# Whole PSUM bank pairs for each transpose task, and new offsets for the left operands of two projections, in a two-layer decoder trunk

## The chip, the cores and the metric

One core of one Trainium2 chip. The metric is the device time of one execution in microseconds (us), the median of the runs; one further execution was taken with the hardware profiler, and its trace is what the text reads.

## The reference

Two decoder layers over 256 tokens with a model width of 1024 (two token tiles of 128), all in float32:

```python
def layer(x, kind):
    x = x + 0.5 * swiglu(rms_norm(x), w_gate, w_up, w_down)   # ffn1, hidden width 2816
    h = rms_norm(x)
    p = h @ w_in                       # q, k, v of two groups of 8 heads of 64
    # kind 0: stick-breaking heads | block-sparse heads (q, k normed, rope)
    # kind 1: forgetting heads (q, k normed, gate log_f) | dilated-window heads (q, k normed, rope)
    o = concat(group_1(p), group_2(p))
    x = x + o @ w_out
    return x + 0.5 * swiglu(rms_norm(x), w_gate, w_up, w_down)   # ffn2
```

With 256 tokens the block-sparse heads see one block, so they are causal softmax attention. Every product is made to nearly float32 accuracy from parts: each operand is a sum of a rounded `hi` and a rest `lo`, and `hi*hi + lo*hi + hi*lo` are added up.

## The kernel before

**Stages.** The feed-forward stage (`ffn`), the mixing stage (`mix`), the feed-forward stage again, twice. Weights stream through: a DMA on the SP queue brings one unit of 128 x 2048 into `raw` (three buffers), ACT rounds each half to `hi` (L238), DVE takes the difference `lo` (L239; nine buffers each), and then come the matmuls (`mm3`, all recorded at L155 in `mm`). The stationary operand is the activations with the features on the partitions, 128 x 128 a matmul; the moving one is the weights, 128 x 512.

**The gate and up projections** run over blocks of 512 or 384 columns, for two token tiles and eight slices of the model width, into an `acc` bank (gate) and a `z` bank (up). The hidden blocks h are transposed, and ACT and DVE split them into `hh` and `hl` (`split_evac`, L251 and L252). **The down projection** (`row_gemm`) takes `hh` and `hl` as the stationary operand. **The mixing stage** projects q, k and v of the one group, then of the other. q and k of the normed heads go through `norm` (ACT square, DVE sum, POOL power, DVE product, and for rope POOL and DVE products: L475 to L488) and are transposed into `qT`, `kT` (L493). Each group then runs over four pairs of heads: scores into two `z` banks (`soft_a`, `stick_a`), a transposition of the weights (`soft_b`, one head a call) or the cumulative sum as a matmul (`stick_b`), and the product with v into the `o` bank (`c`). `out` splits a finished half into `oh`, `ol`, the stationary operand of the out projection.

**The norm of a stage** (`Normed`). After each half of a token tile's residual, the scaled half `xg` is transposed into `xt`. `inverse` takes the norm, and in the mixes it broadcasts the inverse over the partitions by a matmul with a diagonal matrix, into `rb` (L293 to L297).

**PSUM.** Eight banks of 512 columns: three `acc` in turn, one `o`, two `z`, and one tile `tt` of two banks. `slot()` hands out the two halves of 256 columns of `tt` in turn, each half across both banks:

```python
    tt = psum.tile([P, 2, 512], F32, tag="tt", bufs=1, name="tt")
    def slot():
        slots[0] += 1
        c0 = (slots[0] % 2) * 256
        return tt[:, :, c0:c0 + 256]
```

A task is given one half and the next the other half of the same banks. PE waits before it writes one half until the readers of the other are done, as the rows of its waits show.

**The order of the work.** PE's order is written out by hand: `Weave` keeps an estimated clock `pe.t`, and tasks spawned as generators (transposes, norms, groups of heads) are run from within the streams of matmuls when that clock reaches their time. The leads say how long after its inputs' start a task comes: `LEAD_X` for xt, `LEAD_R` and `LEAD_R0` for rope heads, `LEAD_N` for the others, `LEAD_F` for the forget gate, and `PACE` sets the distance of one head pair to the next. The other engines' order is set by the program's scheduler.

**Start.** The first token tile's halves are scaled and transposed one by one, then the second tile's (`second_tile`), between the first gate matmuls.

Of the kernel before, what the change touches and what calls it, by code (L numbers as in the profile page):

```python
# [28 lines left out]
HD = 64  # L29
# [83 lines left out]
def trunk(ctx, tc, a, out):  # L113
# [14 lines left out]
    def nm(s):  # L128
        seen[s] = seen.get(s, 0) + 1
        return f"{s}_{seen[s]}"  # L130
# [4 lines left out]
    def acc():  # L135
        return bank("acc", 3)
# [25 lines left out]

    def transposes(src, n):

        tb = slot()
        for j in range(n):
            for b in range(2):
                r = slice(b * HP, (b + 1) * HP)
                nc.tensor.transpose(tb[:, b, j * HP:(j + 1) * HP], src[r, j * P:(j + 1) * P], ident[r, r])  # L169
            pe.t += 0.06  # L170
        return tb[:, :, :n * HP].rearrange("p b (c t) -> p c b t", t=HP)

# [39 lines left out]
    def rpow(ss, n, width):  # L212

        m = small.tile([P, width], F32, tag=f"ms{width}", name=nm("ms"))
        nc.vector.tensor_scalar(m, ss, 1.0 / n, EPS, op0=ALU.mult, op1=ALU.add)  # L215
        r = small.tile([P, width], F32, tag=f"rp{width}", name=nm("rp"))
        nc.gpsimd.tensor_tensor(r, m, mhalf[:, :width], op=ALU.pow)  # L217
        return r
# [40 lines left out]
    class Normed:  # L259
# [7 lines left out]

        def start(self, t, h, ps=None, scale=1.0, lead=None, gain=None):
            self.ready[t].append(pe.spawn(self.transpose(t, h, ps, scale, lead or LEAD_X[t][h], gain)))

        def transpose(self, t, h, ps, scale, lead, gain):
            tk, sl, kk = slice(t * P, (t + 1) * P), slice(h * 512, (h + 1) * 512), slice(4 * h, 4 * h + 4)
            if ps is not None:
                residual(ps, t, h, scale)
            xg = xpool.tile([P, 512], F32, tag="xg", bufs=2, name=nm("xg"))
            nc.vector.tensor_mul(xg, x[t][:, sl], self.g[:, sl] if gain is None else gain)
            self.xg[t].append(xg)
            yield lead
            split_evac(transposes(xg, 4), self.hi[:, kk, tk], self.lo[:, kk, tk])
            if h == 1:  # L280
                self.rdone[t] = pe.spawn(self.inverse(t, self.xg[t]))

        def inverse(self, t, junk):
# [9 lines left out]
            nc.gpsimd.tensor_mul(diag, ident, self.r[t].to_broadcast([P, P]))  # L293
# [69 lines left out]
    def ffn(layer, wg, wu, wd, xt, done, between=None):  # L363
        with tc.tile_pool(name=nm("ffn"), bufs=1) as fp:
# [19 lines left out]
            def hidden(hs, c0, n):  # L384
                ft, m = c0 // P, n // P
                vs = [transposes(h, m) for h in hs]
                for t, v in enumerate(vs):
                    split_evac(v, hh[:, ft:ft + m, t * P:(t + 1) * P], hl[:, ft:ft + m, t * P:(t + 1) * P])
                yield 0.0
# [53 lines left out]
    def _mix(mp, layer, xt, gains, done):  # L443
# [23 lines left out]

        def project_norm(c0, g, tag, lead=LEAD_R):
            qT = mp.tile([P, 4, SEQ], F32, tag=tag, bufs=2, name=nm(tag))
            tasks = []  # L470
            rope = isinstance(g, tuple)

            def norm(t, ps):
                sq = new("sq")
                nc.scalar.activation(sq, ps, AF.Square, scale=xt.r[t])  # L475
# [4 lines left out]
                nc.vector.scalar_tensor_tensor(heads(qn), heads(ps), xt.r[t],  # L480
                                               r.unsqueeze(2).to_broadcast([P, 8, HD]), op0=ALU.mult, op1=ALU.mult)
                if rope:
                    gc, gs = g
                    o, sw = new("qs"), new("sq")
                    half_swap(lambda u, v: nc.gpsimd.tensor_mul(  # L485
                        heads(sw)[:, :, u], heads(qn)[:, :, v], over_heads(gs[:, t, u])))
                    nc.vector.tensor_mul(heads(o), heads(qn), over_heads(gc[:, t]))  # L487
                    nc.vector.tensor_add(o, o, sw)  # L488
                    yield lead
                else:  # L490
                    o = qn
                    yield LEAD_N
                nc.scalar.activation(halves(qT[:, :, t * P:(t + 1) * P]), transposes(o, 4), AF.Copy,  # L493
                                     scale=1.0 if rope else g)

            token_major(xt, w, c0, acc, lambda t, ps: tasks.append(pe.spawn(norm(t, ps))))
            return qT, tasks

        def forget():
# [12 lines left out]
            pe.join(*xt.rdone)  # L512
            ps = slot()[:, 0]
            for k in range(KT):
# [4 lines left out]
            def rest():  # L519
# [8 lines left out]
                yield LEAD_F  # L528
                tb = slot()[:, 0]
                for t in range(2):  # L530
# [3 lines left out]
                yield 1.0  # L534
                tb = slot()[:, 0]
                mm(tb[:8, 0:P], lg[:, 0], cv("le"), True)
# [23 lines left out]
        class Group:  # L560
# [11 lines left out]
            def run(self, after, pace, other):  # L572
# [5 lines left out]
                for i in range(4 + 2):  # L578
                    if i < 4:
                        a_(i)  # L580
                    if 0 <= i - 1 < 4:
                        b_(2 * (i - 1))
                        b_(2 * (i - 1) + 1)
                    if 0 <= i - 2 < 4:
# [33 lines left out]

            def stick_b(self, h):
                sp, ls = self.z.pop(h)  # L620
                b = slot()
                mm(b[:, 0], cv("suf"), sp[:, 0:256], True)
                mm(b[:, 0, P:], cv("nones"), sp[:, 256:384], False)
                mm(b[:, 1, :P], cv("suf"), sp[:, 256:384], True)
                nc.vector.tensor_add(ls[:, 0:256], ls[:, 0:256], b[:, 0])
                nc.vector.tensor_add(ls[:, 256:], ls[:, 256:], b[:, 1, :P])
                pT = self.pT[h] = new("pT", 384, 4)
                nc.scalar.activation(pT, ls, AF.Exp)

# [35 lines left out]

            def soft_b(self, h):
                tb = transposes(self.z.pop(h), 3)
                pT = self.pT[h] = new("pT", 384, 4)
                nc.vector.tensor_copy(halves(pT.rearrange("p (c t) -> p c t", t=P)), tb)  # L669

            def c(self, p):
                if p % 2 == 0:
                    self.ob = obank()
                c0 = (p % 2) * SEQ
                pTs = [self.pT.pop(2 * p + s) for s in range(2)]
                for t, (r0, r1) in enumerate(((0, 256), (256, 384))):
                    for s in range(2):
                        o = self.ob[s * HD:s * HD + HD, c0 + t * P:c0 + SEQ]
                        mm(o, self.vs[t][:, (2 * p + s) * HD:(2 * p + s + 1) * HD], pTs[s][:, r0:r1],
                           t == 0 and p % 2 == 0, at_once=2)  # L680
# [27 lines left out]
        gq, gk = gains[0]  # L708
        q2, tq = project_norm(cb, gq, "qT", LEAD_R0)
        k2, tk = project_norm(D + cb, gk, "kT")  # L710
# [30 lines left out]
    def second_tile():  # L741
        load_x(1)
        for h in range(2):
            xt.start(1, h, lead=LEAD_0)

    for h in range(2):
        xt.start(0, h, gain=gb[h])
    first_units.extend([lambda: None, second_tile])
# [47 lines left out]
```

## Time and profile before

| | us |
|---|---|
| median of 3 runs (lowest, highest) | 1087.64 (1087.39, 1088.31) |
| the profiled execution | 1086.83 |
| its span, from the first to the last instruction | 1085.0 |
| mixing stage of layer 0, window in the span | 208.0 to 361.2 |
| mixing stage of layer 1, window in the span | 734.0 to 897.8 |
| mean granted clock of PE | 0.983 |

Times in the rows are microseconds from the start of the span, a mean in a group's row is nanoseconds. PE is the matrix engine, PEld its loading of the stationary operand, DVE, ACT and POOL are the vector, scalar and GpSimd engines, SP the engine that issues the weights' DMAs. A row names output and inputs as the program does: `acc<-hi,xt` adds a product of weights and `xt` to an acc bank. `tt<-ident,...` is a transposition by a matmul with the identity. "L169" is a line of the program above. In a row of the timeline, brackets hold the idle time before the instruction and what ended it.

### The profile page before, as it was taken

The numbers are of one execution on the slowest core, as the hardware profiler recorded it, in microseconds if no ns is written. First come the engines' busy times: TensorE is split into PE (matmuls) and PEld (weight loads), VectorE is DVE, ScalarE is ACT, GpSimd is POOL, SyncE is SP. The second block draws the span as 40 slices with busy tenths as digits, with TensorE's granted clock in tenths as the row PEclk, the third lists the DMA queues.
The fourth block names the chain that finished last, engine by engine and source line by source line (L and its number), as shares of the span: only waits on it lengthen the run. The fifth ranks groups of instructions, "written<-read, shape, count | busy, mean of one in ns | idle before, by whom it ended". The sixth has DMA issues, their size and how long they took to land.

```text
span 1085.0 us, 13584 instructions
## 1 busy us (share of the span) xinstructions
PE 1027.7 (95%) x5412; PEld 841.7 (78%) x5412; DVE 611.6 (56%) x825; ACT 497.8 (46%) x682; POOL 76.1 (7%) x91
## 2 busy tenths in 40 slices
PE   5999999898799999999999999998888989999998
PEld 3888988677676788998788899876755767889986
DVE  5554554666756654564475456447667765555541
ACT  6544543454353644453364445335435544544530
POOL 2000000053000000000010000003431000000000
PEclk9999999999999999999999999999999989999999
DMA  9564665452322564565466456534108316454631
GB/s 327 185 210 128 211 229 180 152 178 97 133 101 78 183 216 135 168 241 185 133 224 216 133 170 242 184 131 161 54 17 281 131 57 215 156 169 164 249 118 39
DMA packets 82657, 178.55 MB, mean 165 GB/s; under 512 B 4993, under 2 KB 21665, under 8 KB 82594
## 3 DMA queue, kind: packets, MB, share of 16 engines
q1 hardware_dynamic: 79776, 174.83, 47.2%
q10 hardware_dynamic: 2818, 2.86, 0.8%
q8 instruction: 42, 0.69, 0.3%
q14 instruction: 21, 0.17, 0.0%
HBM read 176.59 MB, written 1.05 MB: 164 GB/s over the span
## 4 chain that ended last, share of the span: by engine, by line
PE 85%; DVE 8%; ACT 2%; issue 2%; POOL 2%; DMA 1%; SPq 0%; DVEq 0%; ACTq 0%
PE acc L155 51%; PE z L155 24%; PE o L155 6%; DVE lo L239 4%; PE tt L169 3%; ACT hi L238 2%; PE tt L155 1%; POOL rp L217 1%; DMA raw<-in_ffn_w_gate 1%; DMA raw<-in_ffn_w_up 1%; DVE pT L669 1%; DVE mx L653 1%; POOL sq L485 1%; DVE qs L487 0%; DVE x L257 0%
## 5 line engine op out<-in xcount | busy, mean ns | idle before, releaser
L239 DVE TENSOR_TENSOR lo<-raw,hi 128x1024 fp32r<-128x1024 f32 (+1 forms) x344 | 403.0, 1182 | 263.8 <-ACT hi L238 255.7
L238 ACT CAST hi<-raw 128x1024 fp32r<-128x1024 f32 (+1 forms) x344 | 344.1, 1010 | 307.5 <-PE z L155 134.1
L155 PE MATMUL acc<-hi,xt 128*128 128x512 f32 (+1 forms) x1088 | 349.1, 391 | 1.8 <-ACT hi L238 1.8
L155 PEld LDWEIGHTS acc<-hi,xt 128*128 128x128 f32 x1088 | 208.3, 193 | 40.0 <-ACT hi L238 2.2
L155 PE MATMUL z<-hi,xt 128*128 128x512 f32 (+1 forms) x768 | 226.5, 371 | 0.0
L155 PE MATMUL acc<-lo,xt 128*128 128x512 f32 (+1 forms) x544 | 210.0, 386 | 0.9 <-DVE lo L239 0.9
L155 PEld LDWEIGHTS z<-hi,xt 128*128 128x128 f32 x768 | 142.5, 188 | 20.0
L155 PE MATMUL z<-lo,xt 128*128 128x512 f32 (+1 forms) x384 | 142.4, 371 | 0.0
L155 PEld LDWEIGHTS acc<-lo,xt 128*128 128x128 f32 x544 | 105.0, 193 | 17.5 <-DVE lo L239 1.8
L155 PE MATMUL acc<-hi,hh 128*128 128x512 f32 x264 | 105.3, 399 | 0.0
L155 PE MATMUL acc<-lo,hh 128*128 128x512 f32 x264 | 104.5, 396 | 0.0
L155 PE MATMUL acc<-hi,hl 128*128 128x512 f32 x264 | 104.2, 395 | 0.0
L155 PEld LDWEIGHTS z<-lo,xt 128*128 128x128 f32 x384 | 72.1, 188 | 9.9
L217 POOL TENSOR_TENSOR rp<-ms,mhalf 128x1 f32<-128x1 f32 (+1 forms) x24 | 30.3, 1261 | 698.0 <-DVE ms L215 692.7
L380 DVE TENSOR_TENSOR h<-z,sg 128x512 f32<-128x512 f32 (+1 forms) x48 | 30.9, 643 | 55.4 <-PE z L155 55.4
L155 PEld LDWEIGHTS acc<-hi,hh 128*128 128x128 f32 x264 | 49.6, 188 | 11.9
L155 PEld LDWEIGHTS acc<-hi,hl 128*128 128x128 f32 x264 | 49.6, 188 | 11.8
L155 PEld LDWEIGHTS acc<-lo,hh 128*128 128x128 f32 x264 | 49.6, 188 | 11.5
L376 ACT ACTIVATE sg<-acc,rp 128x512 f32<-128x512 f32 (+1 forms) x48 | 31.4, 654 | 42.6 <-PE acc L155 42.0
L251 ACT CAST hh<-tt 128x512 fp32r<-128x512 f32 (+1 forms) x48 | 26.5, 551 | 45.5 <-PE tt L169 25.3
L251 ACT CAST xt<-tt 128x512 fp32r<-128x512 f32 x24 | 14.0, 584 | 63.4 <-PE tt L169 62.7
L252 DVE TENSOR_TENSOR hl<-tt,hh 128x512 fp32r<-128x512 f32 (+1 forms) x48 | 31.0, 646 | 20.3 <-ACT hh L251 19.5
(140 smaller groups left out, 840.5 us busy)
## 6 DMA issues: line engine op xcount, KB each, us to landing
raw<-in_ffn_w_down SPq DMA_DIRECT2D x44, 1024.0 KB
raw<-in_ffn_w_up SPq DMA_DIRECT2D x32, 1024.0 KB
raw<-in_ffn_w_gate SPq DMA_DIRECT2D x30, 1024.0 KB
raw<-in_ffn_w_gate SPq DMA_DIRECT2D x16, 768.0 KB
raw<-in_ffn_w_up SPq DMA_DIRECT2D x16, 768.0 KB
raw<-in_w_in_ab SPq DMA_DIRECT2D x12, 1024.0 KB
raw<-in_w_in_cd SPq DMA_DIRECT2D x12, 1024.0 KB
raw<-in_w_out SPq DMA_DIRECT2D x8, 1024.0 KB
```

What stands on the lines that cost most here:

```text
L155: nc.tensor.matmul(o, lhsT, rhs, start=start, stop=stop, skip_group_check=True)
L169: nc.tensor.transpose(tb[:, b, j * HP:(j + 1) * HP], src[r, j * P:(j + 1) * P], ident[r, r])
L217: nc.gpsimd.tensor_tensor(r, m, mhalf[:, :width], op=ALU.pow)
L238: nc.scalar.copy(hi, wi)
L239: nc.vector.tensor_sub(lo, wi, hi.bitcast(F32))
L251: nc.scalar.copy(halves(hi), v)
L252: nc.vector.tensor_sub(halves(lo), v, halves(hi).bitcast(F32))
L376: nc.scalar.activation(sg[t][:, :n], pg[:, :n], AF.Silu, scale=xt.r[t])
L380: nc.vector.tensor_mul(hs[t][:, :n], pu[:, :n], sg[t][:, :n])
L485: half_swap(lambda u, v: nc.gpsimd.tensor_mul(heads(sw)[:, :, u], heads(qn)[:, :, v], over_heads(gs[:, t, u])))
L653: nc.vector.tensor_reduce(m[:, i:i + 1], z[:, r], axis=AX.X, op=ALU.max, negate=True)
L669: nc.vector.tensor_copy(halves(pT.rearrange("p (c t) -> p c t", t=P)), tb)
```

## The change

It has these parts.

- `pair()` takes the place of `slot()`: each task has the whole pair of banks as a tile of its own, with one buffer, and `transposes` takes several sources at once. `soft_b` and `stick_b` do both heads of a pair in one task; `hidden` both token tiles. In `stick_b` each head has a bank and one add of 384 columns instead of two adds. In `soft_b` DVE copies the first head and ACT the second.
- The first stage's two halves of a token tile are transposed as one task (`both`).
- `rb`'s matmul, the forget gate's product and its two small ones go into an `acc` bank.
- The leads: rope 9 (14 for q of the rope heads) to 14 for all, the others 6.5 to 10; PACE of each layer's first group 6.5 to 6.0.
- Small pools for `sq`, `ms` and `rp` go from four buffers to two, and the tile `bf` from 16 to 224 columns. That moves what lies behind them in SBUF: `hh`, `hl` and layer 0's `oh`, `ol` from 512 to 192 in 1024 bytes, layer 1's `oh`, `ol` from 704 to 192. Weights and `xt` stay at 192.

```diff
-LEAD_R, LEAD_R0, LEAD_N, LEAD_F, OVER = 9.0, 14.0, 6.5, 8.0, 4
+LEAD_R, LEAD_N, LEAD_F, OVER = 14.0, 10.0, 8.0, 4
-PACE = ((6.5, 6.0), (6.5, 6.0))
+PACE = ((6.0, 6.0), (6.0, 6.0))
...
-    tt = psum.tile([P, 2, 512], F32, tag="tt", bufs=1, name="tt")
-    slots = [0]
-    def slot():
-        slots[0] += 1
-        c0 = (slots[0] % 2) * 256
-        return tt[:, :, c0:c0 + 256]
+    def pair():
+        return psum.tile([P, 2, 512], F32, tag="tt", bufs=1, name=nm("tt"))
...
-    def transposes(src, n):
-        tb = slot()
+    def transposes(*srcs):
+        tb, n, vs = pair(), 0, []
+        for src in srcs:
...
-        m = small.tile([P, width], F32, tag=f"ms{width}", name=nm("ms"))
+        m = small.tile([P, width], F32, tag=f"ms{width}", bufs=2, name=nm("ms"))
-        r = small.tile([P, width], F32, tag=f"rp{width}", name=nm("rp"))
+        r = small.tile([P, width], F32, tag=f"rp{width}", bufs=2, name=nm("rp"))
...
+        def transpose_both(self, t, gains, lead):
+            for h in range(2):
+                xg = xpool.tile([P, 512], F32, tag="xg", bufs=2, name=nm("xg"))
+                nc.vector.tensor_mul(xg, x[t][:, h * 512:(h + 1) * 512], gains[h])
+                self.xg[t].append(xg)
+            yield lead
+            tk = slice(t * P, (t + 1) * P)
+            for h, v in enumerate(transposes(*self.xg[t])):
+                split_evac(v, self.hi[:, 4 * h:4 * h + 4, tk], self.lo[:, 4 * h:4 * h + 4, tk])
...
-            sq = small.tile([P, 2], F32, tag="sq", name=nm("sq"))
+            sq = small.tile([P, 2], F32, tag="sq", bufs=2, name=nm("sq"))
...
             yield 5.0
-            tb = slot()[:, 0]
+            tb = acc()
             mm(tb[:, :P], ones, diag, True)
...
-            bf = mp.tile([8, 16], F32, name="bf")[:, 0:1]
+            bf = mp.tile([8, 224], F32, name="bf")[:, 0:1]
...
-            ps = slot()[:, 0]
+            ps = acc()
...
+            def stick_b(self, p):
+                b = pair()
+                parts = [self.z.pop(2 * p + s) for s in range(2)]
+                for s, (sp, ls) in enumerate(parts):
+                    mm(b[:, s, 0:256], cv("suf"), sp[:, 0:256], True)
+                    mm(b[:, s, 128:256], cv("nones"), sp[:, 256:384], False)
+                    mm(b[:, s, 256:384], cv("suf"), sp[:, 256:384], False)
+                self.pT[p] = new("pT", 768, 2)
+                for s, (sp, ls) in enumerate(parts):
+                    nc.vector.tensor_add(ls, ls, b[:, s, :384])
+                    nc.scalar.activation(self.pT[p][:, s * 384:(s + 1) * 384], ls, AF.Exp)
...
+            def soft_b(self, p):
+                vs = transposes(*[self.z.pop(2 * p + s) for s in range(2)])
+                self.pT[p] = new("pT", 768, 2)
+                for s, v in enumerate(vs):
+                    pT = self.pT[p][:, s * 384:(s + 1) * 384].rearrange("p (c t) -> p c t", t=P)
+                    (nc.vector.tensor_copy, nc.scalar.copy)[s](halves(pT), v)
```

Three places show what moves on PE. A row is line, operation, output<-inputs and shape; brackets name the engines waited for, and a number behind a name counts the tiles of that name or the instructions of the program.

The first is layer 0's mix, where the first inverse norm is broadcast (`diag_1`) between the down projection (`hh`, `hl`) and the first q matmuls (`xt`). Before:

```order
L155 MATMUL o_1_1245<-lo_70_1520,hh_1_115 128x512
L155 MATMUL o_1_1245<-hi_70_1519,hl_1_116 128x512
L155 MATMUL tt_84<-diag_1_1606,ones_88 128x128 [waits DVE_49,Pool_49]
L155 MATMUL acc_18_1676<-hi_71_1658,xt_3_109 128x512 [waits Activation_49]
L155 MATMUL acc_18_1676<-lo_71_1659,xt_3_109 128x512
```

After:

```order
L150 MATMUL o_1_1252<-lo_70_1527,hh_1_114 128x512
L150 MATMUL o_1_1252<-hi_70_1526,hl_1_115 128x512
L150 MATMUL acc_18_1655<-diag_1_1615,ones_87 128x128 [waits Pool_49]
L150 MATMUL acc_19_1687<-hi_71_1669,xt_3_108 128x512 [waits Activation_49]
L150 MATMUL acc_19_1687<-lo_71_1670,xt_3_108 128x512
```

The broadcast keeps its place, goes to an acc bank and no longer waits for DVE; the q block takes the acc bank after it. Four blocks on, k's second token tile (`acc_23`) now waits for DVE, which reads q's second tile out of the same bank.

The second is where q's second and k's first token tile are transposed (`qs_2` and `qs_3`). Before:

```order
L155 MATMUL acc_22_1901<-hi_82_1897,xt_4_110 128x512
L169 MATMUL tt_84<-ident_87,qs_2_1803 128x64 [waits DVE_49,Activation_49]
L169 MATMUL tt_84<-ident_87,qs_2_1803 128x64 x7
L169 MATMUL tt_84<-ident_87,qs_3_1844 128x64 [waits DVE_49,Activation_49]
L169 MATMUL tt_84<-ident_87,qs_3_1844 128x64 x7
L155 MATMUL acc_22_1901<-hi_82_1897,xt_3_109 128x512
```

After:

```order
L166 MATMUL tt_14_1953<-ident_86,qs_2_1816 128x64 [waits DVE_49,Activation_49]
L166 MATMUL tt_14_1953<-ident_86,qs_2_1816 128x64 x7
L150 MATMUL acc_24_1915<-hi_82_1911,xt_3_108 128x512
...
L150 MATMUL acc_25_1968<-hi_82_1911,xt_4_109 128x512
L166 MATMUL tt_15_1990<-ident_86,qs_3_1857 128x64 [waits DVE_49,Activation_49]
L166 MATMUL tt_15_1990<-ident_86,qs_3_1857 128x64 x7
```

24 matmuls of the v blocks now stand between the two; before, k's transposes stood right behind q's.

The third is a pair of stick heads (`sp_1`, `sp_2`). Before:

```order
L155 MATMUL tt_84<-sp_1_2467,cst_1174 128x256 [waits DMAHW7_49]
L155 MATMUL tt_84<-sp_1_2467,cst_1174 128x128 x2
L155 MATMUL tt_84<-sp_2_2475,cst_1174 128x256 [waits DVE_49]
L155 MATMUL tt_84<-sp_2_2475,cst_1174 128x128 x2
L155 MATMUL acc_29_2513<-hi_91_2415,xt_3_109 128x512
```

After:

```order
L150 MATMUL tt_21_2552<-sp_1_2466,cst_1180 128x256 [waits DMAHW7_49,PE_49]
L150 MATMUL tt_21_2552<-sp_1_2466,cst_1180 128x128 x2
L150 MATMUL tt_21_2552<-sp_2_2474,cst_1180 128x256
L150 MATMUL tt_21_2552<-sp_2_2474,cst_1180 128x128 x2
L150 MATMUL acc_31_2566<-hi_91_2432,xt_3_108 128x512
```

The second head's matmuls no longer wait for a reader of the first head's.

More of the change, by code (lines that the diff above doesn't have):

```diff
@@ L161, in mm3 @@
         mm(ps, xl, wh, False, last)
-    def transposes(src, n):
-        tb = slot()
[L166 to L171, printed above, removed]
+    def transposes(*srcs):
+        tb, n, vs = pair(), 0, []
+        for src in srcs:
+            n0 = n
+            for j in range(src.shape[-1] // P):
+                for b in range(2):
+                    r = slice(b * HP, (b + 1) * HP)
+                    nc.tensor.transpose(tb[:, b, n * HP:(n + 1) * HP], src[r, j * P:(j + 1) * P], ident[r, r])
+                n += 1
+                pe.t += 0.065
+            vs.append(tb[:, :, n0 * HP:n * HP].rearrange("p b (c t) -> p c b t", t=HP))
+        return vs
     def halves(v):
@@ L266, in __init__, with start, transpose, both @@
             self.g, self.r, self.ready, self.rdone, self.xg = g, [None, None], [[], []], [None, None], [[], []]
-        def start(self, t, h, ps=None, scale=1.0, lead=None, gain=None):
-            self.ready[t].append(pe.spawn(self.transpose(t, h, ps, scale, lead or LEAD_X[t][h], gain)))
-        def transpose(self, t, h, ps, scale, lead, gain):
+        def start(self, t, h, ps, scale):
+            self.ready[t].append(pe.spawn(self.transpose(t, h, ps, scale, LEAD_X[t][h])))
+        def transpose(self, t, h, ps, scale, lead):
             tk, sl, kk = slice(t * P, (t + 1) * P), slice(h * 512, (h + 1) * 512), slice(4 * h, 4 * h + 4)
-            if ps is not None:
-                residual(ps, t, h, scale)
+            residual(ps, t, h, scale)
             xg = xpool.tile([P, 512], F32, tag="xg", bufs=2, name=nm("xg"))
-            nc.vector.tensor_mul(xg, x[t][:, sl], self.g[:, sl] if gain is None else gain)
+            nc.vector.tensor_mul(xg, x[t][:, sl], self.g[:, sl])
             self.xg[t].append(xg)
             yield lead
-            split_evac(transposes(xg, 4), self.hi[:, kk, tk], self.lo[:, kk, tk])
+            split_evac(*transposes(xg), self.hi[:, kk, tk], self.lo[:, kk, tk])
             if h == 1:
                 self.rdone[t] = pe.spawn(self.inverse(t, self.xg[t]))
+        def both(self, t, gains, lead):
+            self.ready[t].append(pe.spawn(self.transpose_both(t, gains, lead)))
+        def transpose_both(self, t, gains, lead):
[7 more added lines that the diff above has]
+                split_evac(v, self.hi[:, 4 * h:4 * h + 4, tk], self.lo[:, 4 * h:4 * h + 4, tk])
+            self.rdone[t] = pe.spawn(self.inverse(t, self.xg[t]))
         def inverse(self, t, junk):
-            sq = small.tile([P, 2], F32, tag="sq", name=nm("sq"))
+            sq = small.tile([P, 2], F32, tag="sq", bufs=2, name=nm("sq"))
             for h in range(2):
@@ L385, in hidden @@
                 ft, m = c0 // P, n // P
-                vs = [transposes(h, m) for h in hs]
-                for t, v in enumerate(vs):
+                for t, v in enumerate(transposes(*[h[:, :n] for h in hs])):
                     split_evac(v, hh[:, ft:ft + m, t * P:(t + 1) * P], hl[:, ft:ft + m, t * P:(t + 1) * P])
@@ L466, in project_plain, with project_norm @@
             return qT, []
-        def project_norm(c0, g, tag, lead=LEAD_R):
+        def project_norm(c0, g, tag):
             qT = mp.tile([P, 4, SEQ], F32, tag=tag, bufs=2, name=nm(tag))
@@ L488, in norm @@
                     nc.vector.tensor_add(o, o, sw)
-                    yield lead
+                    yield LEAD_R
                 else:
@@ L492, in norm @@
                     yield LEAD_N
-                nc.scalar.activation(halves(qT[:, :, t * P:(t + 1) * P]), transposes(o, 4), AF.Copy,
+                nc.scalar.activation(halves(qT[:, :, t * P:(t + 1) * P]), transposes(o)[0], AF.Copy,
                                      scale=1.0 if rope else g)
@@ L528, in rest @@
                 yield LEAD_F
-                tb = slot()[:, 0]
+                tb = acc()
                 for t in range(2):
@@ L534, in rest @@
                 yield 1.0
-                tb = slot()[:, 0]
+                tb = acc()
                 mm(tb[:8, 0:P], lg[:, 0], cv("le"), True)
@@ L581, in run @@
                     if 0 <= i - 1 < 4:
-                        b_(2 * (i - 1))
-                        b_(2 * (i - 1) + 1)
+                        b_(i - 1)
                     if 0 <= i - 2 < 4:
@@ L664, in soft_a @@
                     self.z[2 * p + s] = pr
[L666 to L669, printed above, removed]
+            def soft_b(self, p):
[4 more added lines that the diff above has]
+                    (nc.vector.tensor_copy, nc.scalar.copy)[s](halves(pT), v)
             def c(self, p):
@@ L674, in c @@
                 c0 = (p % 2) * SEQ
-                pTs = [self.pT.pop(2 * p + s) for s in range(2)]
+                pT = self.pT.pop(p)
                 for t, (r0, r1) in enumerate(((0, 256), (256, 384))):
@@ L708, in _mix @@
         gq, gk = gains[0]
-        q2, tq = project_norm(cb, gq, "qT", LEAD_R0)
+        q2, tq = project_norm(cb, gq, "qT")
         k2, tk = project_norm(D + cb, gk, "kT")
@@ L742, in second_tile @@
         load_x(1)
[L743 to L747, printed above, removed]
+        xt.both(1, [g0[:, h * 512:(h + 1) * 512] for h in range(2)], LEAD_0)
+    xt.both(0, gb, LEAD_X[0][0])
     first_units.extend([lambda: None, second_tile])
```

12 lines of the change are left out of this document (1 added, 11 removed).

## The prediction

> **What bounds the kernel now.** I read the page first, then a table of busy time by stage, then PE's waits inside the two mixing stages, then the chain and the timeline where the change sits. The page says how much of the span PE works and how much of the chain that ended last is PE's:
>
> ```profile
> PE 1027.7 (95%) x5412; PEld 841.7 (78%) x5412; DVE 611.6 (56%) x825; ACT 497.8 (46%) x682; POOL 76.1 (7%) x91
> PE 85%; DVE 8%; ACT 2%; issue 2%; POOL 2%; DMA 1%; SPq 0%; DVEq 0%; ACTq 0%
> ```
>
> PE is the bound, and its average hides two kinds of stage. In the table by stage the columns are the stretch, its length, busy time of PE, PEld, DVE, ACT, POOL (with counts), PE's granted clock, the DMA share and GB/s; the rows are the start, the first feed-forward stage's gate and up part, and the mixing stages of layers 0 and 1:
>
> ```profile
> 0.00:20.70 20.70, 9.25 (x43) 5.03 (x43) 11.72 (x15) 11.73 (x18) 4.81 (x17) 0.98 0.90 319
> 20.70:145.80 125.10, 125.10 (x647) 108.04 (x648) 68.63 (x73) 63.94 (x76) 3.16 (x11) 0.99 0.57 194
> 208.00:361.20 153.20, 134.25 (x829) 106.36 (x827) 100.89 (x169) 73.83 (x134) 26.28 (x29) 0.97 0.38 130
> 734.00:897.80 163.80, 140.57 (x822) 105.60 (x821) 112.60 (x234) 75.86 (x133) 34.73 (x25) 0.93 0.36 122
> ```
>
> In the feed-forward stage PE never pauses, so only a shorter matmul helps there. In the mixes it stands idle for 19.0 and 23.2 us and its clock is below 1, so there a wait taken away counts. PE's waits in the first mix and, after the "...", in the second (total, times, longest):
>
> ```profile
> PE tt L169 <- DVE pT L669: 6.8, 4, 2.7
> PE tt L169 <- DVE ms L215: 3.9, 1, 3.9
> PE tt L155 <- DVE ls L626: 3.7, 4, 1.6
> PE tt L155 <- DVE xt L252: 3.3, 1, 3.3
> ...
> PE tt L169 <- DVE pT L669: 10.6, 8, 2.7
> PE tt L155 <- DVE xt L252: 3.3, 1, 3.3
> PE tt L169 <- DVE ms L215: 3.0, 1, 3.0
> ```
>
> All of them are PE about to write into tt, the pair of banks that the change hands out differently.
>
> **Operand offsets.** In the program as built, weights and xt lie at 192 in 1024 bytes; hh, hl and layer 0's oh, ol at 512, after the change at 192. Layer 1's oh, ol were at 704, which is 512 from the weights. Two unbroken runs of the same matmul form in the chain (start, length, count), one with the operands 0 or 512 apart (up projection), one 320 or 832 apart (down projection), and the count of the latter's form:
>
> ```profile
> 368.25 10.88 PE z L155 x48
> 1064.49 12.60 PE acc L155 x54
> L155 PE MATMUL acc<-hi,hh 128*128 128x512 f32 x264 | 105.3, 399 | 0.0
> ```
>
> One matmul takes 10.88/48 = 226.7 ns in the first and 12.60/54 = 233.3 ns in the second; the difference is 6.6 ns. The down projection has three such groups of 264 into acc and three of 88 into o, 1056 matmuls: 7.0 us. Layer 0's out projection has 2 x 48 = 96: 0.6 us, by the same difference. PE is never idle in the first of these, so all 7.6 us lie on the path. The bounds are 0 (the offset is not the cause) and 7.6; I take 7.6, because number format, shape and clock are the same in both rows and only the stationary operand's tile differs. The Trainium skill, page "TensorE: Matmul & The Clock Gate", section "Step-by-step: what each phase is for", says that PE reads the streamed operand and the stationary one through two independent SBUF ports, so that one load runs beside the other's stream. By that rule where the two lie could not matter and this term would be 0; the two rows differ by 3%, which the rule does not explain, but no row here changes the place alone.
>
> **The start.** Rows of the timeline (start, length, engine; in brackets the idle time before and what ended it):
>
> ```profile
> 16.25 0.57 PE L169 MATMUL tt<-ident,xg 64*128 64x64 f32 x8 [0.28 <-DVE xt L252]
> 16.98 2.36 DVE L239 TENSOR_TENSOR lo<-raw,hi 128x1024 fp32r<-128x1024 f32 x2
> 19.26 0.68 DVE L252 TENSOR_TENSOR xt<-tt,xt 128x512 fp32r<-128x512 f32 x1
> 20.00 0.69 PE L169 MATMUL tt<-ident,xg 64*128 64x64 f32 x8 [3.18 <-DVE xt L252]
> ```
>
> The second token tile's two halves are transposed one after the other, and the second must wait until DVE, behind two casts, has read the first. Afterwards both stand together at the first place, 8 transposes longer (0.6 us), and the first tile's two halves stand together as well, so that neither waits for a reader. PE goes on at about 16.25 + 0.57 + 0.6 = 17.4 instead of 20.7; that is 3.3, and about 0.3 more since the pair of the first tile is done earlier. I take 3.6; what could eat it is the supply of casts (DVE's two take until 19.34), which would leave 20.7 - 19.3 = 1.4.
>
> **The inverse norm's broadcast (rb).**
>
> ```profile
> 207.52 0.93 POOL L293 TENSOR_TENSOR diag<-ident,rp 128x128 f32<-128x128 f32 x1
> 212.38 0.68 DVE L252 TENSOR_TENSOR xt<-tt,xt 128x512 fp32r<-128x512 f32 x1
> 213.21 0.46 PE L155 MATMUL tt<-diag,ones 128*128 128x128 f32 x2 [3.34 <-DVE xt L252]
> 213.67 5.74 PE acc L155 x18
> 739.99 5.70 PE acc L155 x18
> 216.00:219.50 3.50, 3.50 (x15) 2.49 (x15) 0.00 (x0) 0.00 (x0) 0.00 (x0) 0.73 0.71 209
> ```
>
> The matmul's own input was ready at 208.45; it waited until 212.38 + 0.68 for the reader of the tile's other half. In an acc bank it does not. After the wait the clock was granted at 0.73, and 18 matmuls took 5.74 and 5.70 us instead of 18 x 0.2267 = 4.08. So 3.34 + 1.66 in layer 0 and 3.3 + 1.62 in layer 1 go: 9.9 us. The next step late is the following transpose, which needs that same read (ends 213.06); it comes 18 matmuls after 209.87 (213.21 - 3.34), at 213.95, so it is just covered.
>
> **The heads' norm.** The rope norm of one token tile runs over ACT, DVE and POOL:
>
> ```profile
> 227.15 0.69 ACT L475 ACTIVATE sq<-acc,rp 128x512 f32<-128x512 f32 x1 [0.45 <-issue]
> 233.88 0.75 DVE L480 SCALAR_TENSOR_TENSOR qn<-acc,rp,rp 128x512 f32<-128x512 f32 x1 [1.76 <-POOL rp L217]
> 246.78 0.69 DVE L488 TENSOR_TENSOR qs<-qs,sq 128x512 f32<-128x512 f32 x1
> 247.62 0.46 PE L169 MATMUL tt<-ident,qs 64*128 64x64 f32 x8 [3.88 <-DVE ms L215]
> 248.08 7.28 PE acc L155 x24
> 773.47 7.27 PE acc L155 x24
> ```
>
> The input was ready at 246.78 + 0.69 = 247.47, and PE stood there from 243.74. The lead of this task goes from 9 to 14, and in the new order the k tile's transposes come 24 matmuls (24 x 0.2267 = 5.4 us) later, at about 249.2: covered by 1.7. That frees 3.88 and 3.0, and the low clock behind them, 7.28 and 7.27 instead of 24 x 0.2267 = 5.44: 1.8 each; 10.5 together. Against it: rb now takes turns in the ring of three acc banks, so k's second tile takes the bank of q's second tile, which is free when qn has read it, 233.88 + 0.75 - 227.15 = 7.5 us after it ended; 24 matmuls and some 0.8 us of transposes and rb lie between, 6.2. The trace has no such wait; it is worth 0 to 2 us a layer and I take 1.3, 2.6 for both. Net 7.9.
>
> **Both heads at once.** A soft task and a stick task, each with the second head waiting for the first one's reader:
>
> ```profile
> 309.16 0.28 DVE L626 TENSOR_TENSOR ls<-ls,tt 128x128 f32<-128x128 f32 x1
> 309.50 1.14 PE L155 MATMUL tt<-sp,cst 128*128 128x256 f32 x6 [0.71 <-DVE ls L626]
> 791.35 0.55 DVE L669 COPY pT<-tt 128x384 f32<-128x384 f32 x1
> 791.95 0.40 PE L169 MATMUL tt<-ident,t 64*128 64x64 f32 x6 [0.86 <-DVE pT L669]
> ```
>
> With both heads in one pair of banks nobody reads in between. Layer 0: 6.8 + 3.7 = 10.5 us, less about 1.5 where a task now meets the one before it (0 to 3): 9.0. Layer 1: 10.6, but its last group has little work beside it, and there PE waits for the softmax itself:
>
> ```profile
> 871.61 0.40 PE L169 MATMUL tt<-ident,t 64*128 64x64 f32 x6 [2.17 <-DVE pT L669]
> 875.15 0.58 PE L169 MATMUL tt<-ident,t 64*128 64x64 f32 x6 [1.24 <-DVE pT L669]
> ```
>
> These 3.4 stay, and I leave the longest of the others, 2.7, in place too, since its successor in the new order stands equally close behind its softmax: 4.5. One copy of each soft pair moves from DVE to ACT, 12 x 0.55 = 6.6 us, hidden by ACT's 73.83 of 153.20 and 75.86 of 163.80 us; stick's eight adds of 0.28 fall away on DVE, off the path. In the feed-forward stage both tiles' hidden transposes already ran as one task, some 20 us from the next: nothing.
>
> **Sum.** 7.6 + 3.6 + 9.9 + 7.9 + 9.0 + 4.5 = 42.5. The profiled execution took 1086.83 us (span 1085.0); 1086.83 - 42.5 = 1044.3, and the median of the runs is 0.8 above that execution: 1045.1.
>
> **The rivals.** *The offset does nothing* (with the skill's two ports): all but its term stays, 1045.1 + 7.6 = 1052.7. For it: down and up differ in more than the place, hh is written by ACT shortly before. Against: layer 1's out projection, at 512, has no such surplus.
>
> *The waits come back elsewhere.* One pair of banks now serves each task whole, and acc carries rb. If half of what the mixes give (9.9 + 7.9 + 9.0 + 4.5 = 31.3) returns as waits for qn, for ACT's second copy or for the pair, it is 1045.1 + 15.7 = 1060.8. For it: the norm's 7.5 us against 6.2. Against: DVE and ACT are at 66% and 48% in the first mix.
>
> *Slower: the hand-over of the pair.* With a single buffer no task can fill the other half while the first is read. The trace's price for one such hand-over is 17.5/12 = 1.46 us:
>
> ```profile
> PE tt L169 <- DVE pT L669: 17.5, 12, 2.7
> ```
>
> The program has 44 such tasks in and around the mixes; if each met its predecessor, 64.2 us come against 42.5 saved, 1045.1 + 64.2 = 1109.3. It decides once 30 of the 44 stand within 1.5 us of the one before. The new order has 20 or more matmuls (4.5 us) between most of them, so I give it little.
>
> *The change does not do what it says:* the other half was free in time anyway and PE's waits are put down to the wrong releaser; then the same inputs end last and only noise is left, 1087.6.
>
> **How the numbers follow.** Forecast 0.68, offset nothing 0.09, waits come back 0.13, slower 0.07, no effect 0.03. The low end takes away what I left in place: 2.6 + 1.5 + 3.4 + 2.7 = 10.2, 1034.9, so 1035. The high end is the rival with half the waits, 1060.8, with the start's lost 2.2 on top: 1063. The first three cases hold 0.90; what their terms could miss by makes it about 8 in 10. Faster by over 0.2% (about 2.2 us, what a measurement of this kernel tells from no change): 0.68 + 0.09 + 0.13 = 0.90; same 0.03; slower 0.07.
>
> **What would show it.** Offset: the down projection's long run in the chain falls from 233.3 to 226.7 ns a matmul. Start: PE's row at 20.00 is gone and the up projection begins some 3.6 us earlier. rb and heads: no wait over 2 us of PE for xt or ms in the mixes, and a clock of 1.00 behind them. Pairs: one wait at most per task. New: acc waiting for qn, 1 to 2 us a layer. I am wrong if the mixes' PE idle time stays above 10 us each, or if the feed-forward stages, which should change by the offset alone, change otherwise.

## The result and the profile after

The changed kernel took 1044.82 us in the median of four runs, 1087.91 before; the ratio is 0.9593 (95% interval 0.9558 to 0.9628). One of the four, 1256.89 us at a granted clock of 0.753, is left out of the ratio and lifts that median; the other three took 1041.21, 1042.60 and 1047.03 us. The profiled execution took 1041.21 us, its span is 1039.4 against 1085.0, 45.6 less; 42.5 was forecast.

The page of the changed kernel, engines and the chain that ended last:

```profile
PE 1007.6 (97%) x5412; PEld 833.9 (80%) x5412; DVE 604.5 (58%) x805; ACT 503.0 (48%) x694; POOL 81.5 (8%) x91
PE 90%; DVE 4%; ACT 2%; DMA 2%; issue 1%; POOL 1%; SPq 0%; ACTq 0%; POOLq 0%
```

To place the 45.6 us I cut both spans at the same work: at the first up projection, at the end of each gate and up part, and at the end of the down projection's last run of 30 matmuls into acc. From that run to the next stage's first up projection is what I call a mix's stretch from here on; it includes the down projection's tail and the next stage's first gate block. The table of busy time has for it, before, layers 0 and 1:

```profile
198.32:368.25 169.93, 150.97 (x911) 119.56 (x912) 109.58 (x183) 84.48 (x150) 28.50 (x32) 0.97 0.37 124
724.64:904.84 180.20, 156.97 (x904) 118.61 (x904) 121.05 (x248) 86.19 (x148) 36.92 (x28) 0.93 0.34 115
```

and after:

```profile
191.58:338.90 147.32, 144.52 (x911) 116.36 (x912) 106.33 (x171) 86.67 (x154) 31.77 (x32) 1.00 0.42 143
692.33:860.92 168.59, 151.20 (x904) 115.54 (x904) 117.16 (x240) 89.60 (x156) 36.77 (x28) 0.96 0.36 123
```

Layer 0's mix gave 22.6 us and its granted clock is 1.00; layer 1's gave 11.6, its clock is 0.96, and PE still stands idle for 17.4 us in it. PE's waits in the two stretches after (layer 0's first two, a "...", layer 1's first five):

```profile
PE z L150 <- ACT t L671: 1.4, 2, 1.3
PE tt L166 <- DVE xt L251: 1.1, 1, 1.1
...
PE tt L166 <- ACT pT L683: 6.8, 2, 4.9
PE z L150 <- ACT t L671: 2.5, 2, 2.3
PE tt L166 <- DVE t L675: 2.4, 3, 1.0
PE acc L150 <- ACT hi L237: 1.8, 1, 1.8
PE acc L150 <- DVE lo L238: 1.8, 1, 1.8
```

No wait for ms or for rb's reader is left, and none of acc for qn, which I had expected. New is the first of layer 1: ACT's copy of a pair's second head. The timeline of the changed kernel shows the longer of its two waits:

```profile
770.68 1.99 ACT L237 CAST hi<-raw 128x1024 fp32r<-128x1024 f32 x2 [2.31 <-DMA raw<-in_w_in_cd]
772.94 0.47 ACT L683 COPY pT<-tt 128x384 f32<-128x384 f32 x1
773.47 0.56 PE L166 MATMUL tt<-ident,qn 64*128 64x64 f32 x8 [4.92 <-ACT pT L683]
```

ACT's small copy stands in its queue behind two casts of weights, and these behind a DMA that landed late; PE wants the pair of banks for the next transposes and waits for all three.

The chain has the two matmul forms of the prediction again, up and down projection:

```profile
338.90 10.88 PE z L150 x48
1019.38 12.24 PE acc L150 x54
```

12.24/54 = 226.7 ns: both the same now. The first up projection in the chain, before and after:

```profile
31.71 10.88 PE z L155 x48
```

```profile
26.38 10.88 PE z L150 x48
```

The start is 31.71 - 26.38 = 5.3 us shorter. In the timeline of the changed kernel the second tile's transposes stand together, with a wait of 0.58 us:

```profile
15.92 0.72 PE L166 MATMUL tt<-ident,xg 64*128 64x64 f32 x16 [0.58 <-DVE ms L214]
```

Before, the table of busy time has behind the wait of 3.18 us:

```profile
20.69:23.50 2.81, 2.81 (x7) 2.23 (x8) 1.22 (x2) 2.30 (x3) 1.51 (x7) 0.53 1.03 394
```

The clock stood at 0.53; I had priced the wait there and not the clock. The 5.3 us hold for these two executions: in other runs with the change's start the up projection began up to 3.1 us later (last section).

The differences by stretch are 5.3 (start), 22.6 and 11.6 (mixes), and in the four down projections outside them 1.42, 1.59, 1.42 and 1.70. Together they are the 45.6; gate and up parts agree within 0.03.

### The profile page after: what moved, and what is told of

It reads as the page before. It is cut to its first block, busy times and chain, and to the rows that moved or that the text cites. A ratio compares the mean times of both kernels' runs of the same rounds, so it can differ in the third digit from the quotient of the medians.

```text
span 1039.4 us, 13568 instructions
## 1 busy us (share of the span) xinstructions
PE 1007.6 (97%) x5412; PEld 833.9 (80%) x5412; DVE 604.5 (58%) x805; ACT 503.0 (48%) x694; POOL 81.5 (8%) x91
## 4 chain that ended last, share of the span: by engine, by line
PE 90%; DVE 4%; ACT 2%; DMA 2%; issue 1%; POOL 1%; SPq 0%; ACTq 0%; POOLq 0%
PE acc L150 55%; PE z L150 24%; PE o L150 7%; PE tt L166 3%; DVE lo L238 2%; ACT hi L237 1%; DMA hg<-in_g_k_b 1%; DMA raw<-in_w_in_cd 1%; PE tt L150 1%; POOL rp L216 0%; SPq L565 0%; DVE t L675 0%; ACT t L671 0%; DVE mx L665 0%; DVE hss L489 0%
## 5 line engine op out<-in xcount | busy, mean ns | idle before, releaser
L150 PE MATMUL acc<-hi,xt 128*128 128x512 f32 (+1 forms) x1088 | 343.1, 385 | 5.6 <-ACT xt L250 3.9
L150 PEld LDWEIGHTS acc<-hi,xt 128*128 128x128 f32 x1088 | 204.0, 189 | 42.5 <-ACT xt L250 4.1
L150 PE MATMUL acc<-lo,xt 128*128 128x512 f32 (+1 forms) x544 | 206.5, 380 | 1.8 <-DVE lo L238 1.8
L250 ACT CAST hh<-tt 128x512 fp32r<-128x512 f32 (+1 forms) x48 | 26.5, 551 | 45.6 <-PE tt L166 25.3
```

The lines of the kernel that those rows point to most:

```text
L150: nc.tensor.matmul(o, lhsT, rhs, start=start, stop=stop, skip_group_check=True)
L250: nc.scalar.copy(halves(hi), v)
```

## The experiments

My theory was that each term of the sum can be found again by undoing its part alone, and the main rivals were an offset without effect, and waits that come back elsewhere. Stretches are compared, since the start moved by up to 3 us from run to run (last section). Each stretch is read from one profiled execution. Three runs leave the order of layer 1's mix as the change has it (the change, the four offsets, the halves apart); they took 168.59, 168.05 and 170.02 us for it, so a difference below 2 us there says nothing. Layer 0's has two lengths, 1.4 us apart (last section).

**The offset alone**, the kernel before with the sizes of the small pools and of `bf`:

```diff
-        m = small.tile([P, width], F32, tag=f"ms{width}", name=nm("ms"))
+        m = small.tile([P, width], F32, tag=f"ms{width}", bufs=2, name=nm("ms"))
...
-            bf = mp.tile([8, 16], F32, name="bf")[:, 0:1]
+            bf = mp.tile([8, 224], F32, name="bf")[:, 0:1]
```

> The kernel before with only the pool and tile sizes that move hh, hl, oh and ol to 192; order and banks as before. If the offset costs the 6.6 ns a matmul: down projections at 226.7 ns, total 7 to 8 us less than before (about 1080). Rival, the place does not matter and the change's order or banks made the matmuls shorter: 233.3 ns and 1087 to 1088.

1081.43 us against 1090.65 of the kernel before on the same chip, ratio 0.9918 (0.9903 to 0.9932). Its chain has

```profile
1059.59 12.24 PE acc L155 x54
```

226.7 ns, with the order and banks of before. By stretches the down projections are shorter by the same 1.42, 1.59, 1.42 and 1.70, the mixes (169.52 and 179.83 us) by 0.41 and 0.37: 6.9 together. The medians differ by 9.2; where the other 2.3 us lie, these profiles do not show. The rival falls. The Trainium skill's two independent read ports (page "TensorE: Matmul & The Clock Gate", section "Step-by-step: what each phase is for") do not make the place indifferent: the trace differs by 6.6 ns.

**Four offsets**, a pad ahead of `hh` in the changed kernel, 320, 256, 128 and 64 bytes in the four stages:

```diff
+            n_pad = {"ffn_1": 80, "ffn_2": 64, "ffn_3": 32, "ffn_4": 16}[f"ffn_{seen['ffn']}"]
+            fp.tile([P, n_pad], F32, name=nm("pad"))
             hh = fp.tile([P, FT, SEQ], F32R, name=nm("hh"))
```

> The changed kernel with a pad ahead of hh in each feed-forward stage, so that hh and hl lie 320, 256, 128 and 64 bytes behind the weights modulo 1024 in the four down projections in turn; nothing else. Theory of the place modulo 512: all four slower, 233 ns at 320 and somewhere between 226.7 and 234 at the others, total up by 2 to 7 us (1043 to 1048 against 1041). Rival, only the alignment to 512 or 1024 of the tile itself or something else counts: 226.7 ns in all four, total unchanged.

A run of 15 matmuls from each down projection, in that order, from the chain:

```profile
149.01 3.50 PE acc L150 x15
463.03 3.40 PE acc L150 x15
651.40 3.50 PE acc L150 x15
986.11 3.50 PE acc L150 x15
```

233.3 ns at 320, 128 and 64, but 226.7 at 256. Both expectations missed one thing: not 512 but 256 bytes is the period, within what was tried (0, 64, 128, 256, 320, and 512 in layer 1's out projection before). The total, 1047.63 us in one run, lies in the 1043 to 1048 of the theory. In every run the weights stayed at 192 and only the stationary operand moved. So the runs do not tell whether its distance from the weights counts or its own address modulo 256.

**rb in the pair of banks**:

```diff
             yield 5.0
-            tb = acc()
+            tb = pair()[:, 0]
             mm(tb[:, :P], ones, diag, True)
```

> The changed kernel with rb's broadcast taking the pair of banks instead of an acc bank. Theory: PE waits again for the reader of the last transposed xt, 3 us each in both mixes, and the granted clock falls behind it, 1.7 us each: total up by 6 to 10 (1047 to 1051). Rival, the new order has moved that reader forward, so the bank did not matter: total 1041 to 1043.

The waits are back, here layer 0's and layer 1's, with the stretches of the mixes:

```profile
PE tt L150 <- DVE xt L251: 3.4, 1, 3.4
...
PE tt L150 <- DVE xt L251: 3.7, 1, 3.7
```

```profile
194.18:346.18 152.00, 146.02 (x911) 117.49 (x912) 107.23 (x171) 86.44 (x154) 31.42 (x32) 0.99 0.41 139
699.65:872.94 173.29, 153.56 (x903) 117.52 (x904) 118.13 (x240) 89.48 (x156) 36.89 (x28) 0.94 0.35 119
```

152.00 - 147.32 = 4.7 and 173.29 - 168.59 = 4.7: 9.4 us, against 9.9 forecast. The total, 1053.26 us in one run, lies above the 1047 to 1051 expected: its up projection also began 2.6 us later than the changed kernel's.

**The old leads** (rope 9, 14 for q, others 6.5, pace 6.5):

```diff
-LEAD_R, LEAD_N, LEAD_F, OVER = 14.0, 10.0, 8.0, 4
+LEAD_R, LEAD_R0, LEAD_N, LEAD_F, OVER = 9.0, 14.0, 6.5, 8.0, 4
-PACE = ((6.0, 6.0), (6.0, 6.0))
+PACE = ((6.5, 6.0), (6.5, 6.0))
```

> The changed kernel with the leads and the pace of before (rope 9, 14 for q, others 6.5, pace 6.5). Theory, the later place of the heads' transposes took away the waits on the norm and the low clock behind them: layer 0's mix 4 to 6 us longer than in the change, layer 1's 3 to 5, with PE waiting over 2 us for a norm in each. Rival, the whole pair alone removes them: mixes unchanged within 1 us.

Its wait for the norm in layer 0, and the two stretches:

```profile
PE tt L166 <- DVE ms L214: 3.6, 1, 3.6
```

```profile
191.61:343.48 151.87, 146.87 (x911) 118.01 (x912) 106.32 (x171) 86.13 (x154) 28.80 (x32) 0.98 0.41 139
696.93:860.18 163.25, 150.89 (x903) 115.10 (x904) 117.32 (x240) 89.27 (x156) 36.67 (x28) 0.96 0.37 127
```

In layer 0 the leads give 4.55 us, as expected. In layer 1 the old ones are better by 5.3, and PE's wait for `ms` there is 1.3 us and not the 3.0 of before: neither theory had that. The total was 1040.50 us in one run.

**One head a task**, soft and stick:

```diff
-                vs = transposes(*[self.z.pop(2 * p + s) for s in range(2)])
                 self.pT[p] = new("pT", 768, 2)
-                for s, v in enumerate(vs):
+                for s in range(2):
+                    v = transposes(self.z.pop(2 * p + s))[0]
...
                 for s, (sp, ls) in enumerate(parts):
+                    b = pair()
```

> The changed kernel with soft and stick tasks that take the pair of banks for one head each, so that the second head waits for the first one's readers. Theory: layer 0's mix 8 to 11 us longer; layer 1's 3 to 6 longer. Second theory, in layer 1 the late weights set the time and the joint tasks give nothing there: layer 1's mix within 1.5 us, with layer 0's longer as before. Rival, the joint tasks give nothing at all: both within 1 us.

The waits that came back (two of layer 0, one of layer 1), and the stretches:

```profile
PE tt L166 <- DVE pT L682: 6.5, 4, 2.6
PE tt L150 <- DVE ls L638: 3.6, 4, 1.6
...
PE tt L166 <- DVE pT L682: 12.0, 8, 2.7
```

```profile
191.58:350.55 158.97, 147.52 (x911) 118.11 (x912) 107.34 (x171) 86.91 (x154) 31.77 (x32) 0.99 0.38 133
703.97:879.96 175.99, 153.29 (x903) 116.60 (x904) 118.63 (x240) 90.22 (x156) 36.75 (x28) 0.94 0.34 117
```

11.65 and 7.4 us longer, more than the 9.0 and 4.5 of the sum and than expected. In layer 0, idle time grew by 8.65 us, 11.45 against 2.80, and PE's busy time by 3.0 (147.52 against 144.52) for the same matmuls. Part of that is clock: behind a wait of 2.64 us it stood at 0.73 from 256 to 260 us and at 0.84 from 260 to 264, which makes 4 x 0.27 + 4 x 0.16 = 1.7 us by estimate. In layer 1 idle time grew by 5.3 and busy time by 2.1.

**Both copies on DVE**:

```diff
-                    (nc.vector.tensor_copy, nc.scalar.copy)[s](halves(pT), v)
+                    nc.vector.tensor_copy(halves(pT), v)
```

> The changed kernel with both heads' soft copies on DVE, as it was before the change. Theory, ACT's second copy stands behind weight casts and holds the pair of banks: PE's waits of 4.9 and 1.9 us for ACT's pT in layer 1 go, total 4 to 8 us less than the change (1033 to 1037). Rival, the order of the work there leaves nothing and DVE is as late: the waits show under DVE's pT instead, total 1040 to 1044.

1046.45 us, ratio 0.9600 to before (0.9583 to 0.9616), no better than the change. Layer 1's mix is 171.67 instead of 168.59; ACT's pT is gone from its waits, and these two are now the largest:

```profile
PE tt L166 <- DVE t L675: 4.0, 3, 2.7
PE acc L150 <- DVE lo L238: 3.3, 2, 2.9
```

My theory of a copy on the wrong engine fell: the wait changes its name. The rival is not met either, as DVE's pT is not among these waits and the total lies above its 1040 to 1044. ACT's rows above say why the wait could change its name: what was late there was the weights' DMA. On SP's queue the forget gate's eight DMAs of `rows` stand ahead of the last three weight units of the layer's projections, and `rows` and `cl` hold two of the three weight buffers. In the changed kernel:

```profile
760.12 5.14 SPq L565 DMA_DIRECT2D rows<-cl  x8
765.36 2.46 SPq L231 DMA_DIRECT2D raw<-in_w_in_cd  x3
```

The queue had stood for 27.0 us until DVE had written `cl`; the first of the three units is the one that ACT casts at 770.68.

**The forget gate off the weight buffers**, `cl` in a tile of its own, the rows sent right into `ck` and `cq` (ACT's two casts of `rows` fall away with it, and `bf` has 32 columns here):

```diff
-                cl = raw_p.tile([8, 4, SEQ], F32, tag="raw", name="cl")
+                cl = mp.tile([8, 4, SEQ], F32R, name="cl")
...
-                            nc.sync.dma_start(rows[b0 + 2 * i + j:b0 + 2 * i + j + 1, i],
-                                              cl[s::2, 2 * i + j])
-                for i, dst in enumerate((ck, cq)):
-                    nc.scalar.copy(dst, rows[:, i])
+                            nc.sync.dma_start((ck, cq)[i][b0 + 2 * i + j:b0 + 2 * i + j + 1].bitcast(F32),
+                                              cl[s::2, 2 * i + j].bitcast(F32))
```

> The changed kernel, layer 1's forget gate without the two of three weight buffers that its rows took: cl in a tile of its own, the rows sent by DMA right into ck and cq without a cast. Theory, layer 1's mix waits for weights that come late behind those rows, and ACT's and DVE's small copies stand behind the casts of these weights: layer 1's mix 6 to 12 us shorter than in the change (168.6), the waits for ACT's pT, hi and lo gone. Rival, DVE is full in that stretch and sets its time: within 2 us; or ck and cq come late behind the weights in SP's queue: longer.

1037.07 us, ratio 0.9523 (0.9507 to 0.9539). Layer 1's mix is 163.11, 5.5 shorter, a little under the range I gave; hi and lo are gone from its waits, and ACT's pT has fallen from 6.8 to 2.2. SP's queue issued the last weight unit of the projections by 690.91 + 55.44 = 746.35 us, ahead of the forget gate's DMAs, which start at 762.94, and not behind them. Two of its waits, and SP's row:

```profile
PE tt L166 <- DVE t L674: 4.9, 4, 1.6
...
PE tt L166 <- ACT pT L682: 2.2, 2, 1.5
...
690.91 55.44 SPq L231 DMA_DIRECT2D raw<-in_w_in_cd  x9
```

**Which lead costs layer 1 its 5.3 us**: two runs, each with a part of the old leads there. The first sets `LEAD_N` back:

```diff
-                    yield LEAD_N
+                    yield 6.5
```

> The changed kernel with the lead of layer 1's un-roped heads back at 6.5 (10 in the change); rope leads and pace as in the change. With all leads of before, layer 1's mix was 163.25 against 168.59. Theory, the un-roped heads' transposes come right behind a soft task and wait for its copies because of their later place: 163 to 165. Rival, the rope lead or the pace has it: 168 to 169.

The second sets k's rope lead and the first group's pace back, in layer 1 alone:

```diff
-PACE = ((6.0, 6.0), (6.0, 6.0))
+PACE = ((6.0, 6.0), (6.5, 6.0))
...
-        k2, tk = project_norm(D + cb, gk, "kT")
+        k2, tk = project_norm(D + cb, gk, "kT", 9.0 if layer else LEAD_R)
```

> The changed kernel with layer 1's rope lead for k (9) and its first group's pace (6.5) of before; the un-roped heads' lead stays at 10. By the theory of the un-roped lead layer 1's mix stays at 167 to 169; by its rival it falls to 163 to 165. Layer 0's mix as in the change, 147 to 149.

Layer 1's mix took 169.39 and 168.31: neither part alone does it, so neither the theory of the un-roped lead nor its rival holds. Its largest wait in the first, and in the second:

```profile
PE tt L166 <- DVE t L675: 8.7, 2, 5.3
```

```profile
PE tt L166 <- ACT pT L683: 5.8, 1, 5.8
```

Once more the stall has another name and the stretch the same length.

**Both gains of layer 1 together**: the change's leads in layer 0, those of before in layer 1, the forget gate off the weight buffers (the edits above, no new one).

> The changed kernel with its own leads in layer 0, those of before in layer 1, and the forget gate off the weight buffers. If the two gains in layer 1 (5.3 by the leads, 5.5 by the forget gate) are of one cause, the same late weights, its mix is 161 to 164 and the total 1033 to 1037; if they add up, 157 to 159 and 1028 to 1032.

1026.60 us against 1088.72 before on the same chip, ratio 0.9446 (0.9417 to 0.9476), faster than both kernels. Layer 1's mix and its largest wait:

```profile
692.87:844.82 151.95, 146.03 (x903) 112.70 (x904) 116.06 (x240) 87.81 (x154) 36.10 (x31) 0.99 0.41 136
```

```profile
PE tt L166 <- DVE t L674: 3.4, 1, 3.4
```

16.6 us shorter than in the change, where 5.3 and 5.5 were to be had one by one: more than either theory. With the late weights present, the old leads gain 168.59 - 163.25 = 5.3; with them gone, 163.11 - 151.95 = 11.2. My reading, which no further run shows, is that part of what a better order saves is spent on waiting for the weights.

**The first stage's halves apart**:

```diff
-            for h, v in enumerate(transposes(*self.xg[t])):
+            for h in range(2):
+                v = transposes(self.xg[t][h])[0]
```

> The changed kernel with the first stage's two halves of a token tile transposed in a pair of banks each. Theory: the up projection begins 3 to 6 us later than with both halves together on the same chip (28.6 to 29.0 in the runs here), and every later stage is as long as in the change. Rival, the first weights' arrival sets the start: under 1 us later.

The wait at the start is there again in the timeline, and the chain's first up projection begins at 33.61 us:

```profile
21.04 0.69 PE L166 MATMUL tt<-ident,xg 64*128 64x64 f32 x8 [4.10 <-DVE xt L251]
```

```profile
33.61 10.88 PE z L150 x48
```

Runs with both halves together began it at 26.37 to 29.48, on the same chip at 26.37, 26.38 and 29.29: 4.3 to 7.2 us. The mixes were to be as long as in the change and took 1.4 us more each, 148.73 and 170.02, which is within what they moved by unchanged.

## Why the prediction was right, point by point

| term | forecast, us | measured, us | by |
|---|---|---|---|
| offset | 7.6 | 6.9 | the offset alone |
| start | 3.6 | 5.3 (4.3 to 7.2) | the two profiles (halves apart) |
| rb in an acc bank | 9.9 | 9.4 | rb in the pair |
| heads' norm, layer 0 | 4.4 | 4.55 | the old leads |
| heads' norm, layer 1 | 3.5 | -5.3 | the old leads |
| both heads at once, layer 0 | 9.0 | 11.65 | one head a task |
| both heads at once, layer 1 | 4.5 | 7.4 | one head a task |
| sum | 42.5 | 39.9 (directly 45.6) | |

The mechanisms hold but for the leads in layer 1. The total is 3 us off, and that close partly by luck: 8.8 us too much for the norm of layer 1 stand against 5.55 too little for the pairs, 1.7 for the start, and 5.7 that belong to no single part when the parts are undone one at a time. Of these 5.7, 4.4 lie in layer 1's mix (4.7 - 5.3 + 7.4 + 0.4 = 7.2 against 11.6). The forget gate's move into `acc` banks was undone in no run.

**Offset.** Right in that the place counts, and in the size: 6.6 ns a matmul in every down projection. Layer 0's mix gave 0.4 of the 0.9 that its out projection and the down projection's tail should have; where the other 0.5 went stays open.

**Start.** Right in the wait; mis-sized by the clock behind it: seven matmuls took the 2.81 us of the row from before at 20.69, where 1.6 would have done. Of the ten runs with the change's start, six began the up projection at 28.6 to 29.5 us, only 2.2 to 3.1 before the 31.71 of the kernel before (33.16 in the offset alone), so 3.6 is as good a figure as 5.3.

**rb.** Right, the clock included.

**Heads' norm.** In layer 0 right in sum: of the 4.55 us, 2.2 are idle time and 2.35 are PE's busy time, that is clock. The 1.3 set aside for the acc ring did not show; in its place the change has the 1.4 us for which z waits for ACT's t, a wait that the run with the old leads does not have. The step "that frees 3.88 and 3.0" failed in layer 1. The 3.0 did go, but with the old leads only 1.3 of it comes back. With the new leads PE waited elsewhere instead, in a stretch where weights were late, under whatever name stood last: ACT's pT, DVE's t, hi or lo. The late weights are shown as one part of that, 5.5 us by themselves. Which of the moved tasks costs the 5.3 stays open, since neither lead set back alone gave any of it. My second rival, waits that come back elsewhere, is what happened in layer 1.

**Both heads at once.** Right, and too low by 5.55 us. In layer 0 the waits have the size forecast, 8.65 us of idle time against 9.0, and the 3.0 of busy time come on top. I priced the waits and took no clock for them. The prediction's own pattern for rb and the norm, first the wait and then 1.66 and 1.8 us of clock behind it, belonged here too. In layer 1 I also misread a row. The wait of 2.17 us at 871.61, left in place as one for the softmax, was one for DVE's copy of the first head, as the row says; the second head's softmax was done at 865.69 + 0.55 = 866.24:

```profile
865.69 0.55 DVE L663 TENSOR_SCALAR t<-t,l 128x128 f32<-128x128 f32 x2
```

**Rivals.** The offset without effect is excluded by two runs. The hand-over of the pair costs 1.46 us only where tasks stand close; the profile after shows PE waiting for a pair's readers 6.8 + 1.0 us in layer 1 and 1.1 us in layer 0, so its point of decision was never near.

**The tests I set.** No wait over 2 us for xt or ms, the 226.7 ns, the start's row, the gate and up parts unchanged: as said. The clock of 1.00 in the mixes: so in layer 0, 0.96 in layer 1. acc waiting for qn: absent. PE idle above 10 us in each mix was to prove me wrong: layer 0 has 2.8, but layer 1 has 17.4, and the total came out because other terms were larger. As a forecast of layer 1's mix, 12.9 us and the offset's 0.4, against 11.6 measured, the sum is close; as an account of it, it was wrong in the leads.

## What to carry to other kernels

A wait that only changes its name between variants, while the stretch keeps its length, is not the cause: look for the input that is late in all of them, here, in part, a weight's DMA behind small DMAs on the same queue and in the same buffers. Price a PE wait with the clock behind it. And look where the operands of a long stream of matmuls lie: bringing the stationary one to the place of the moving one modulo 256 bytes took a few buffer counts and the size of one small tile here and gave 6.9 us.

## What the runs showed of the hardware

The place of the stationary operand sets the length of a 128 x 512 matmul in this kernel. With the moving one at 192 modulo 1024, it is 226.7 ns at 0, 256 and 512 bytes from there and 233.3 at 64, 128 and 320. The moving one was never shifted.

The clock can fall behind shorter gaps than I thought. In the run with the forget gate off the weight buffers, a gap in layer 0's mix and the clock some 2 us after it:

```profile
274.77:276.23 1.46, 0.20 (x2) 0.10 (x1) 1.46 (x3) 1.46 (x5) 0.00 (x0) 1.00 0.37 149
277.90:281.20 3.30, 3.30 (x20) 2.19 (x20) 1.78 (x6) 2.26 (x6) 0.00 (x0) 0.52 0.76 285
```

The changed kernel has the same gap and kept its clock at 1.00 in the seven microseconds behind it. The mix's stretch is 147.3 us in the one case and 148.8 in the other. Of the seven runs with the change's own layer 0, four took 147.3 or 147.4 and three 148.7 or 148.8; the other two of the three have the slow piece behind this gap too, at a clock of 0.50 (halves apart from 283 to 285 us, `LEAD_N` set back from 278 to 280). The Trainium skill, page "TensorE: Matmul & The Clock Gate", section "What's actually happening", has a window of about 3.4 us that runs freely, and an idle one of which lowers the clock. The length of the slow piece, 3.3 us, agrees with one window, and so does the chance in it; that a gap of 1.4 us is enough does not follow from an idle window, since by the profile PE was busy for more than half of any 3.4 us there (1.95 us from 274.50 to 277.90).

The start moved from run to run, too: the first up projection of kernels with the change's start began at 26.4 to 26.9 us in some runs and at 28.6 to 29.5 in others. In one of the late ones, matmuls followed each other at (19.52 - 18.24)/3 = 427 ns until 21.6 us, in the changed kernel's profile at (17.83 - 17.13)/3 = 233 ns from 17.1 on:

```profile
18.24 1.05 PE L150 MATMUL acc<-hi,xt 128*128 128x512 f32 x2
19.52 1.05 PE L150 MATMUL acc<-hi,xt 128*128 128x512 f32 x2
```

```profile
17.13 0.62 PE L150 MATMUL acc<-hi,xt 128*128 128x512 f32 x2
17.83 0.62 PE L150 MATMUL acc<-hi,xt 128*128 128x512 f32 x2
```

The column of the granted clock shows 1.00 in both, so at the very start the matmuls' own spacing is the better clock.
